# A fixed order on TensorE for attention: scores of two heads over all tokens in one run, transposes and value products in runs between projections

## The chip, the cores and the metric

The kernel runs on one core of a Trainium2 chip. The metric is the device time of one execution in microseconds (us). Engines are named TensorE (PE in the profile, its weight loads PEld), VectorE (DVE), ScalarE (ACT), GpSimd (POOL) and SyncE (SP). The change moves work on TensorE and, through a list scheduler, on the others.

## What is computed

A decoder trunk of two layers over 512 tokens of width 1024. The first layer is a gated short convolution with its feed-forward part, the second an attention layer with its own. The change lies in the attention layer alone. Cut to that:

```python
def dilated_attention_mixer(x, positions, k_sh, v_sh, w_q, w_o):
    q = rope((x @ w_q).reshape(B, S, N_BRANCHES * N_HEADS, HEAD_DIM), positions)
    for g, (window, dilation) in enumerate(((128, 1), (512, 4), (2048, 16))):
        o, lse = dilated_branch(q[:, :, g], k_sh[:, :, g], v_sh[:, :, g], window, dilation)
    wts = softmax(stack(lses), axis=0)
    return (sum over branches of wts * o) @ w_o
```

Each of the three branches has 16 heads of 64. `dilated_branch` takes the scores of a query with the keys of its own residue class and window, masks them, and returns the softmax-weighted values and the log of the sum of exponentials. k and v come from the same hidden state by another normalisation gain and another weight matrix, `w_kv`. All is float32.

## The kernel before, in words

**Products in three parts.** A float32 product is made of three TensorE products: activations and weights are split in a high and a low part (`split`, L88 to L91: a cast `wh` on ScalarE, a subtraction `wl` on VectorE), and high by high, high by low and low by high are added up in PSUM. `load` (L95) fetches 1 MB of weight into a tile `raw` of a pool with two buffers; `parts` (L101) multiplies it in place by the norm's gain (L110, VectorE, in two pieces per half, so four per `raw`), then splits it. `wh` and `wl` have six buffers each.

**The projections.** `feature_mm` (L119, matmul L137) runs 24 steps for a pair of outputs, 48 matmuls of 512 columns. `rope_mms` (L534) does this for q and for k of one branch, four heads at a time, and `rope` (L518) turns the result: eight narrow ScalarE copies `sw` (L527, L528), and three VectorE steps per output (L529 to L531). `sw` takes one of four buffers of tag "t".

**The heads.** There are four groups of four heads. A group's `Heads` object (L553) has these steps:
- `scores` (L568): fp32 matmuls q by k of 64 rows for two token blocks and both heads of a pair, into two PSUM banks of tag "at" (L580); a VectorE operation adds the mask, writes p and takes the maximum (L588); after the second two blocks `nm` (L595) and the exp on ScalarE (L598). `part` 1 holds branches 1 and 2, which share a token order, `part` 0 holds branch 0.
- `values` (L636): the projection v of one branch in two pieces of 48 matmuls of 256 columns each (L649), then copies to SBUF on ScalarE (L657, L662), 16 narrow ones for branch 0.
- `factors` (L601): the statistics of the two parts go through DRAM to the other part's token order and back (GpSimd DMAs, L612 to L616); VectorE makes the common maximum `mx` (L624) and from it the factor `f` (L625 to L633).
- `transposed` (L667): VectorE scales p by f (L676), TensorE transposes 128 x 128 tiles `tr` (L679), ScalarE copies them to `trs` (L681), again of tag "t".
- `times_v` (L684): fp32 value products into one bank `o` for both heads (L708), later copied out (L717).
- `units` (L721): per head pair, part and two token blocks a unit, that is a transposition of both heads; the products of a unit follow one unit later (`rest`).

**What sets the order.** The group loop (L749) does the six projection pairs of a group, builds the scores as a list `todo`, makes the six value pieces, then puts the units in `todo`. `fill` (L744) takes two items off the list: it is called after each value piece, so that scores stand between values, and after each projection pair, so that the units of a group stand between the projections of the next. The last group's units stand between steps of the output projection (`wo_step`, L505, `token_mm`, L175). PSUM has eight banks, four of tag "mm" for projections, values and output, four of tag "at". A scheduler then puts each engine's instructions in a row by a simulated time line, keeping data dependencies, buffers and the edges set with `tc.issue_after`; in this version it is free to cut a run of scores or transposes and put full-array matmuls between.

Of the kernel before, what the change touches and what calls it, by code (L numbers as in the profile page):

```python
# [38 lines left out]
def trunk(  # L39
# [78 lines left out]

    def feature_mm(jobs, t0, t1, attn):  # L119
# [12 lines left out]
        if t1 - t0 < NT:  # L132

            todo.sort(key=lambda kp: kp[1])
        for i, (k, p) in enumerate(todo):
            for ps, (_, (wh, wl)) in zip(outs, jobs):
                nc.tensor.matmul(ps, (wh, wl, wh)[p][:, k, :], x[p == 2][:, k],  # L137
                                 start=i == 0, stop=i == len(todo) - 1)

# [7 lines left out]

    def feature_mms(makers, between=None, attn=False, marks=((), ())):

# [3 lines left out]
        if between is None:  # L153
            pairs = [m() for m in makers]
            for i in range(0, len(pairs), 2):
                feature_mm(pairs[i:i + 2], 0, NT, attn)
            return [ps for ps, _ in pairs]
# [16 lines left out]

    def token_mm(outs, ah, al, wh, wl, first, last):  # L175
# [327 lines left out]

    def wo_step(k, tt, n):
        wh, wl = ws[4 * n + k // 2]  # L505
        return token_mm([ys[tt][n]], xh[:, tt, k, :], xl[:, tt, k, :],
                        [wh[:, k % 2, :]], [wl[:, k % 2, :]], k == 0, k == KT - 1)

    with ExitStack() as inner:
# [24 lines left out]
        def rope_mms(g, i, rest, fill):  # L534
# [4 lines left out]
            for src, gain in ((w_q[0], gq), (w_kv, gkv)):  # L539
                tag = "at" if ms and rest else "mm"  # L540
                ms += makers(tag, load_cols(src, c0), gain)
                if not rest:
                    d += [rope(ps, f"qk{g}", g) for ps in feature_mms(ms[-2:], None, True)]
                    fill()
# [8 lines left out]
        class Heads:  # L553
# [13 lines left out]

            def scores(self, part, pr, b2):  # L568

                st = self.st[part]  # L570
                ps = [bank("at", "s").rearrange("p (b k) -> p b k", b=2) for _ in range(2)]
                for b in (b2, b2 + 1):
                    for e in range(2):
# [4 lines left out]
                        for h2 in range(2):  # L578
                            rw = slice(64 * h2, 64 * h2 + 64)
                            nc.tensor.matmul(  # L580
                                ps[h2][:, b - b2, e * P:(e + 1) * P],
                                q[pr][rw, b * P:(b + 1) * P], k[pr][rw, kb * P:(kb + 1) * P],
                                start=True, stop=True)
                    lo = 128 if part == 0 and b == 0 else 0
                    mask = (maskA, maskB)[part]
                    for h2 in range(2):
                        hh = 2 * pr + h2
                        nc.vector.tensor_tensor_reduce(  # L588
                            self.p(part, hh, b), ps[h2][:, b - b2, lo:], mask[:, lo:],
                            1.0, -3.0e38, ALU.add, ALU.max, st[:, b, hh, 0:1])  # L590
                if b2 == 0:
                    return
                for hh in (2 * pr, 2 * pr + 1):
# [42 lines left out]
            def values(self, g):  # L636
# [7 lines left out]
                def piece(n):  # L644
                    for k in range(KT):
                        wh, wl = (x[:, k % 4, :] for x in w[k // 4])
                        for p in range(3):
                            for m in range(2):
                                nc.tensor.matmul(  # L649
                                    ps[m][:, n, :], (zh, zh, zl)[p][:, k, 2 * m + n],  # L650
                                    (wh, wl, wh)[p],
                                    start=k == 0 and p == 0, stop=k == KT - 1 and p == 2)
                    if n:
# [13 lines left out]
            def transposed(self, pr, part, hh, b2):  # L667
# [5 lines left out]
                for b in (b2, b2 + 1):  # L673
# [4 lines left out]
                    for e in range(lo, 256, P):  # L678
                        nc.tensor.transpose(  # L679
                            tr[:, b - b2, e:e + P], p[:, e - lo:e - lo + P], ident)  # L680
                nc.scalar.copy(trs.rearrange("p a b -> p (a b)")[:, lo0:], trf[:, lo0:])  # L681
                return trs

            def times_v(self, pr, part, b2, trs):  # L684
# [4 lines left out]
                o = self.o[pr]  # L689
                mark = None  # L690
                for b in (b2, b2 + 1):
                    for e in range(2):
                        if part == 0 and b + e == 0:
                            continue
                        for hh in range(2):
# [10 lines left out]
                            first = new and b == 0 and e == 0  # L706
                            with tc.issue_after(mark) if mark else nullcontext():
                                m = nc.tensor.matmul(  # L708
                                    out, v, rhs, start=first, stop=part == 0 and e == 1,
                                    skip_group_check=True).ins  # L710
                            if first:
                                mark = m
                if part == 1 or b2 == 0:
# [7 lines left out]
            def units(self):  # L721

                def unit(pr, part, b2):
# [5 lines left out]
                return [lambda a=(pr, part, b2): unit(*a)  # L729
                        for pr in range(2) for part in (1, 0) for b2 in (0, 2)] + [self.rest]  # L730

            def rest(self):
                what, trs = self.flight.pop(0)
                self.times_v(*what, trs)

# [8 lines left out]
        def fill():  # L744
            for f in todo[:2]:
                f()
            del todo[:2]

        for i in range(NG):  # L749
            qk = [rope_mms(g, i, pending.rest() if i == 0 and g == 0 else {}, fill)  # L750
                  for g in range(NB)]
            for f in todo:
                f()
# [4 lines left out]
            todo = [lambda a=(part, pr, b2): heads.scores(*a)  # L758
                    for part in range(2) for pr in range(2) for b2 in (0, 2)]
            for g in range(NB):  # L760
                for piece in heads.values(g):
                    piece()
                    fill()
            heads.factors()
            todo = heads.units()
        load_wo(0)
# [4 lines left out]
        steps = [(k, tt) for k in range(6) for tt in range(NT)]  # L771
        for n, f in enumerate(todo):
            for s in steps[3 * n:3 * n + 3]:
                wo_step(*s, 0)
            f()
# [79 lines left out]
```

## Time and profile before

| what | before |
|---|---|
| runs (three), median | 1523.56 us |
| lowest and highest run | 1521.35 and 1524.08 us |
| profiled execution: its time, its span | 1523.93 us, 1522.1 us |
| mean granted TensorE clock | 0.994 of full speed |
| TensorE busy | 1495.3 us (98%), 8158 matmul records |
| VectorE busy | 745.4 us (49%) |
| ScalarE busy | 616.4 us (40%) |
| GpSimd busy | 108.1 us (7%) |
| DMA | 137.43 MB, mean 90 GB/s |

The span is the part of the execution between the first and the last instruction that the profiler records. Matmuls overlap in the array, so a row's duration is longer than its distance to the next row, and times below are taken from start to start. An fp32 matmul (scores, value products) leaves two records, any other one. Lines named L... are those of the kernel before.

### The profile page before, as it was taken

What the parts mean: (1) busy time and instruction counts of PE and PEld (TensorE: products, weight loads), DVE (VectorE), ACT (ScalarE), POOL (GpSimd) and SP (SyncE); (2) the same over time, 40 slices, a digit from 0 to 9 for tenths busy, and PEclk for the clock granted to TensorE, in tenths of its full rate; (3) what the DMA queues carried; (4) which work ended last, traced back from release to release, by engine and by line L of the source; (5) the groups of instructions that cost most, each with busy time, mean ns of one, the idle gap of its engine ahead of it and who ended that gap; (6) DMA issues with size and microseconds to landing.
All of it is one profiled execution on the core that took longest, in us unless ns stands there. A gap on an engine that the chain in (4) does not pass through costs nothing.

```text
span 1522.1 us, 20115 instructions
## 1 busy us (share of the span) xinstructions
PE 1495.3 (98%) x8158; PEld 1262.2 (83%) x8158; DVE 745.4 (49%) x1328; ACT 616.4 (40%) x1137; POOL 108.1 (7%) x247
## 2 busy tenths in 40 slices
PE   8999999999999998999999999999998999999997
PEld 7888888888888887898788889889877888888886
DVE  5644453323234366776667566765554322223333
ACT  4323342212123244664666557557553221212321
POOL 2000320000000051000001001000023000000001
PEclk9999999999999999999999999999999999999999
DMA  6333123133323312322112222212040323332311
GB/s 210 111 112 110 56 94 127 62 106 111 124 87 107 111 38 74 111 85 80 61 58 85 84 73 69 84 56 84 30 138 24 124 76 111 111 109 99 111 56 56
DMA packets 109330, 137.43 MB, mean 90 GB/s; under 512 B 3469, under 2 KB 97973, under 8 KB 109238
## 3 DMA queue, kind: packets, MB, share of 16 engines
q1 hardware_dynamic: 107958, 135.89, 27.1%
q8 instruction: 64, 1.05, 0.3%
q0 software_dynamic: 1280, 0.26, 0.2%
q14 instruction: 28, 0.23, 0.0%
HBM read 133.92 MB, written 2.23 MB: 89 GB/s over the span
## 4 chain that ended last, share of the span: by engine, by line
PE 68%; issue 24%; POOL 5%; DVE 1%; ACT 1%; DMA 0%; SPq 0%; DVEq 0%; ACTq 0%; POOLq 0%
PE mmf L137 27%; PE atf L137 14%; PE vps L649 10%; PE s L580 3%; PE o L708 2%; PE tr L679 2%; POOL t L203 1%; POOL a L197 1%; POOL yi L205 1%; POOL q L204 1%; POOL t L206 1%; PE y L182 1%; PE y L180 1%; PE y L178 1%; DVE hn L228 0%
## 5 line engine op out<-in xcount | busy, mean ns | idle before, releaser
L91 DVE TENSOR_TENSOR wl<-raw,wh 128x1024 fp32r<-128x1024 f32 x244 | 292.7, 1222 | 70.7 <-ACT wh L90 70.4
L90 ACT CAST wh<-raw 128x1024 fp32r<-128x1024 f32 x244 | 246.7, 1047 | 100.7 <-PE atf L137 43.1
L137 PE MATMUL mmf<-xh,wh 128*128 128x512 f32 (+1 forms) x848 | 277.4, 380 | 0.2 <-ACT xh L90 0.2
L137 PE MATMUL mmf<-xl,wh 128*128 128x512 f32 (+1 forms) x848 | 271.2, 374 | 0.0
L137 PE MATMUL mmf<-xh,wl 128*128 128x512 f32 (+1 forms) x848 | 271.0, 374 | 0.0
L137 PE MATMUL atf<-xh,wh 128*128 128x512 f32 (+1 forms) x560 | 181.8, 368 | 0.0
L137 PE MATMUL atf<-xl,wh 128*128 128x512 f32 (+1 forms) x560 | 180.1, 365 | 0.0
L137 PEld LDWEIGHTS mmf<-xh,wh 128*128 128x128 f32 x848 | 154.7, 191 | 30.6 <-issue 2.1
L137 PE MATMUL atf<-xh,wl 128*128 128x512 f32 (+1 forms) x560 | 180.0, 365 | 0.0
L362 DVE TENSOR_TENSOR act<-atf,s 128x512 f32<-128x512 f32 x44 | 30.5, 692 | 304.1 <-ACT s L361 304.1
L137 PEld LDWEIGHTS mmf<-xl,wh 128*128 128x128 f32 x848 | 153.2, 188 | 28.8 <-issue 0.9
L137 PEld LDWEIGHTS mmf<-xh,wl 128*128 128x128 f32 x848 | 153.5, 189 | 27.7
L361 ACT ACTIVATE s<-mmf 128x512 f32<-128x512 f32 x44 | 26.3, 598 | 336.3 <-PE mmf L137 336.3
L110 DVE TENSOR_TENSOR raw<-raw,cols 128x512 f32<-128x512 f32 x144 | 90.2, 686 | 78.6 <-DMA raw<-in_w_kv 56.2
L137 PEld LDWEIGHTS atf<-xh,wh 128*128 128x128 f32 x560 | 100.6, 191 | 17.0
L137 PEld LDWEIGHTS atf<-xl,wh 128*128 128x128 f32 x560 | 99.6, 189 | 16.8
L137 PEld LDWEIGHTS atf<-xh,wl 128*128 128x128 f32 x560 | 99.5, 189 | 16.8
L527 ACT COPY sw<-mmf 32x512 f32<-32x512 f32 x92 | 53.3, 579 | 79.4 <-PE mmf L137 72.2
L649 PE MATMUL vps<-wh,xh 128*128 128x256 f32 x384 | 81.1, 289 | 0.0
L649 PE MATMUL vps<-wh,xl 128*128 128x256 f32 x384 | 79.3, 286 | 0.0
L649 PE MATMUL vps<-wl,xh 128*128 128x256 f32 x384 | 79.1, 285 | 0.0
L91 DVE TENSOR_TENSOR al<-act,ah 128x512 fp32r<-128x512 f32 x44 | 30.2, 691 | 93.9 <-ACT ah L90 93.9
(192 smaller groups left out, 2058.6 us busy)
## 6 DMA issues: line engine op xcount, KB each, us to landing
raw<-in_ffn_w_gate_up SPq DMA_DIRECT2D x44, 1024.0 KB, 7.5
raw<-in_w_kv SPq DMA_DIRECT2D x24, 1024.0 KB, 5.2
raw<-in_ffn_w_down SPq DMA_DIRECT2D x22, 1024.0 KB, 4.9
raw<-in_conv_w_in SPq DMA_DIRECT2D x12, 1024.0 KB, 5.2
raw<-in_w_q SPq DMA_DIRECT2D x12, 1024.0 KB, 5.2
raw<-in_conv_w_out SPq DMA_DIRECT2D x4, 1024.0 KB, 4.8
raw<-in_w_o SPq DMA_DIRECT2D x4, 1024.0 KB, 5.0
h<-in_x SPq DMA_DIRECT2D x4, 512.0 KB, 8.9
```

The lines of the kernel that those rows point to most:

```text
L90: return [nc.scalar.copy(hi, src).ins, nc.vector.tensor_tensor(lo, src, hi.bitcast(F32), ALU.subtract).ins]
L91: nc.vector.tensor_tensor(lo, src, hi.bitcast(F32), ALU.subtract).ins]
L110: nc.vector.tensor_tensor(src[:, ks], src[:, ks], g.broadcast_to([P, a // 2, b]), ALU.mult)
L137: nc.tensor.matmul(ps, (wh, wl, wh)[p][:, k, :], x[p == 2][:, k], start=i == 0, stop=i == len(todo) - 1)
L178: nc.tensor.matmul(o, ah, wh[i], start=first, stop=False)
L361: nc.scalar.activation(s, ps[2 * j], AF.Silu)
L362: nc.vector.tensor_tensor(act[2 * c + j], ps[2 * j + 1], s, ALU.mult)
L527: nc.scalar.copy(w[s:s + 32], y[s + 32:s + 64])
L580: nc.tensor.matmul(ps[h2][:, b - b2, e * P:(e + 1) * P], q[pr][rw, b * P:(b + 1) * P], k[pr][rw, kb * P:(kb + 1) * P], start=True, stop=True)
L649: nc.tensor.matmul(ps[m][:, n, :], (zh, zh, zl)[p][:, k, 2 * m + n], (wh, wl, wh)[p], start=k == 0 and p == 0, stop=k == KT - 1 and p == 2)
L679: nc.tensor.transpose(tr[:, b - b2, e:e + P], p[:, e - lo:e - lo + P], ident)
L708: m = nc.tensor.matmul(out, v, rhs, start=first, stop=part == 0 and e == 1, skip_group_check=True).ins
```

## The change

1. `strict` issues a TensorE instruction and adds an edge from the strict one issued before it. All of the projections with `fill`, the scores, value pieces, transposes, value products and the output steps between the last units go through it, so that TensorE keeps the order in which the program is written. (All those instructions then bear line L124.)
2. `scores` does all four token blocks of a head pair in one go, 14 matmuls for part 0 and 16 for part 1, and takes all four banks of tag "at" for it.
3. `fill` takes one item instead of two. It is called ahead of each value piece instead of behind it, and also in the middle of each projection pair, ahead of its 25th matmul.
4. A unit's transposes are made one unit at a time, and value products in pairs of units: before an even unit's transposes come the products of the two units before.
5. `token_mm`, where it is strict, does the three products of an output in a row.

Cut to its core:

```diff
+    traced = []
+    def strict(op, *args, **kwargs):
+        with tc.issue_after(traced[0]) if traced else nullcontext():
+            traced[:] = [op(*args, **kwargs).ins]
...
+    def feature_mm(jobs, t0, t1, attn, fill=None):
...
         for i, (k, p) in enumerate(todo):
+            if fill and i == len(todo) // 2:
+                fill()
             for ps, (_, (wh, wl)) in zip(outs, jobs):
...
+                if fill:
+                    strict(nc.tensor.matmul, *args, **kwargs)
...
-            def scores(self, part, pr, b2):
+            def scores(self, part, pr):
...
-                ps = [bank("at", "s").rearrange("p (b k) -> p b k", b=2) for _ in range(2)]
-                for b in (b2, b2 + 1):
+                banks = [[bank("at", "s").rearrange("p (b k) -> p b k", b=2) for _ in range(2)]
+                         for _ in range(2)]
+                for b in range(NT):
...
-                    self.flight.append(((pr, part, b2), [
-                        self.transposed(pr, part, hh, b2) for hh in (2 * pr, 2 * pr + 1)]))
-                    if len(self.flight) > 1:
+                def unit(n, what):
+                    if n % 2 == 0:
                         self.rest()
+                    if what:
+                        pr, part, b2 = what
+                        self.flight.append((what, [
+                            self.transposed(pr, part, hh, b2) for hh in (2 * pr, 2 * pr + 1)]))
...
             def rest(self):
-                what, trs = self.flight.pop(0)
-                self.times_v(*what, trs)
+                for what, trs in self.flight:
+                    self.times_v(*what, trs)
+                self.flight.clear()
...
         def fill():
-            for f in todo[:2]:
-                f()
-            del todo[:2]
+            if todo:
+                todo.pop(0)()
...
             for g in range(NB):
                 for piece in heads.values(g):
+                    fill()
                     piece()
-                    fill()
```

How the order of instructions changes is shown at three places. In these rows `s<-qk` is a score, `vps` a value matmul, `mmf` a projection matmul, `tr` a transpose of p, `o<-trs` a value product; "x6" is six alike in a row, and numbers behind a name tell tiles apart.

TensorE, the score phase of the third group, before (the first rows lie in the second value piece):

```order
L649 MATMUL vps<-wh,xl 128x256 x2
L649 MATMUL vps<-wh,xh 128x256
L580 MATMUL s<-qk_6750,qk_6623 128x128 x6
L649 MATMUL vps<-wh,xh 128x256
L649 MATMUL vps<-wl,xh 128x256 x2
L649 MATMUL vps<-wh,xl 128x256 x2
L580 MATMUL s<-qk_6759,qk_6632 128x128
L649 MATMUL vps<-wh,xh 128x256 x2
```

After, from the last projection matmul to the value piece behind the second run:

```order
L124 MATMUL mmf<-xl,wh 128x512 x2
L124 MATMUL s<-qk_6774,qk_6641 128x128 x14
L124 MATMUL vps<-wh,xh 128x256 x2
...
L124 MATMUL vps<-wh,xl 128x256 x2
L124 MATMUL s<-qk_6783,qk_6650 128x128 x14
L124 MATMUL vps<-wh,xh 128x256 x2
```

The scores of a head pair were cut into several runs with value matmuls between them; now the 14 stand together, with a whole value piece behind them. Over the four groups, 51 score runs have become 16.

TensorE, the first units of the third group, before:

```order
L137 MATMUL mmf<-xh,wh 128x512 x2
L679 MATMUL tr<-ident,p_7256 128x128 x16
L137 MATMUL mmf<-xh,wl 128x512 x2
...
L137 MATMUL mmf<-xh,wl 128x512 x2
L708 MATMUL o<-trs,v_7478 64x128 x2
L708 MATMUL o<-trs,v_7673 64x128 x2
L708 MATMUL o<-trs,v_7478 64x128 x2
L708 MATMUL o<-trs,v_7673 64x128 x2
L137 MATMUL mmf<-xl,wh 128x512 x2
...
L137 MATMUL mmf<-xl,wh 128x512 x2
L679 MATMUL tr<-ident,p_7255 128x128 x3
L137 MATMUL mmf<-xh,wh 128x512 x2
```

After:

```order
L124 MATMUL mmf<-xl,wh 128x512 x2
L124 MATMUL tr<-ident,p_7256 128x128 x8
L124 MATMUL mmf<-xh,wh 128x512 x2
...
L124 MATMUL mmf<-xl,wh 128x512 x2
L124 MATMUL tr<-ident,p_7256 128x128 x8
L124 MATMUL mmf<-xh,wh 128x512 x2
...
L124 MATMUL mmf<-xl,wh 128x512 x2
L124 MATMUL o<-trs,v_7478 64x128 x2
L124 MATMUL o<-trs,v_7673 64x128 x2
...
L124 MATMUL o<-trs,v_7673 64x128 x2
L124 MATMUL tr<-ident,p_7255 128x128 x6
```

Each unit's eight transposes now stand by themselves, half a projection pair apart, and the products of two units stand together (two times 16 records), directly followed by the next transposes. The first transposes come 24 projection matmuls after the last value matmul.

VectorE, behind the last `nm` of the second group, before:

```order
L110 TENSOR_TENSOR raw_6952<-raw_6952,cols_73 128x4x128 [waits DMAHW4_49]
L110 TENSOR_TENSOR raw_6952<-raw_6952,cols_73 128x4x128 x3
L91 TENSOR_TENSOR wl_6820<-raw_6816,wh_6819 128x1024 [waits Activation_49]
L91 TENSOR_TENSOR wl_6827<-raw_6816,wh_6826 128x1024 [waits PE_49,Activation_49]
L624 TENSOR_TENSOR mx_6531<-st0_6000,ot0_6517 128x16 [waits DMASW2_49,DMASW3_49,DMASW1_49,DMASW0_49]
L624 TENSOR_TENSOR mx_6545<-st1_6001,ot1_6518 128x16 [waits DMASW6_49]
L625 TENSOR_TENSOR ea_6532<-st0_6000,mx_6531 128x16 [waits DVE_49]
...
L629 TENSOR_TENSOR f0_6534<-ea_6532,st0_6000 128x16 [waits Activation_49]
```

After:

```order
L91 TENSOR_TENSOR wl_6681<-raw_6677,wh_6680 128x1024 [waits Activation_49]
L91 TENSOR_TENSOR wl_6688<-raw_6677,wh_6687 128x1024 [waits PE_49,Activation_49]
L110 TENSOR_TENSOR raw_6943<-raw_6943,cols_73 128x4x128 [waits DMAHW4_49,DVE_49]
L110 TENSOR_TENSOR raw_6943<-raw_6943,cols_73 128x4x128 x2
L644 TENSOR_TENSOR mx_6531<-st0_6000,ot0_6517 128x16 [waits DMASW2_49,DMASW3_49,DMASW1_49,DMASW0_49]
L644 TENSOR_TENSOR mx_6545<-st1_6001,ot1_6518 128x16 [waits DMASW6_49]
L110 TENSOR_TENSOR raw_6943<-raw_6943,cols_73 128x4x128
L91 TENSOR_TENSOR wl_6814<-raw_6810,wh_6813 128x1024 [waits Activation_49]
...
L646 TENSOR_TENSOR eb_6547<-ot1_6518,mx_6545 128x16
```

Here `raw_6943` is the weight loaded into the buffer of `raw_6677`, after `wl_6688` has read that. Three of its four gain pieces now stand between `wl_6688` and `mx`, and the fourth with a `wl` between `mx` and `ea`; before, `mx` came right behind the two `wl`.

## Rows read from the trace of the kernel before

**Rows 1.** Windows view: stretch, length, busy by engine (records), clock, DMA.

```profile
639.88:770.61 130.73, 130.73 (x877) 111.18 (x876) 89.42 (x213) 80.20 (x173) 6.08 (x10) 1.00 0.25 78
900.04:947.52 47.48, 47.48 (x409) 44.37 (x408) 33.26 (x101) 34.44 (x97) 3.77 (x7) 1.00 0.23 73
947.52:1029.54 82.02, 82.02 (x471) 66.64 (x469) 53.92 (x110) 45.15 (x75) 2.13 (x4) 1.00 0.23 75
1029.54:1077.02 47.48, 47.48 (x410) 44.18 (x408) 25.72 (x87) 36.80 (x100) 4.59 (x8) 1.00 0.23 74
```

**Rows 2.** Timeline of TensorE, scores among value matmuls: start, busy us, instruction, count.

```profile
917.54 0.72 PE L580 MATMUL s<-qk,qk 64*128 64x128 f32 x8
918.19 0.38 PE L649 MATMUL vps<-wh,xh 128*128 128x256 f32 x1
...
920.57 0.40 PE L649 MATMUL vps<-wl,xh 128*128 128x256 f32 x2
920.89 1.16 PE L580 MATMUL s<-qk,qk 64*128 64x128 f32 x16
921.99 0.50 PE L649 MATMUL vps<-wh,xl 128*128 128x256 f32 x2
922.33 0.40 PE L649 MATMUL vps<-wh,xh 128*128 128x256 f32 x2
```

**Rows 3.** Timeline of TensorE, transposes and value products among projection matmuls.

```profile
958.89 1.91 PE L679 MATMUL tr<-ident,p 128*128 128x128 f32 x16
960.56 0.71 PE L137 MATMUL mmf<-xh,wl 128*128 128x512 f32 x2
...
968.81 0.61 PE L137 MATMUL mmf<-xh,wl 128*128 128x512 f32 x2
969.36 1.09 PE L708 MATMUL o<-trs,v 128*64 128x128 f32 x16
970.38 0.73 PE L137 MATMUL mmf<-xl,wh 128*128 128x512 f32 x2
970.95 0.62 PE L137 MATMUL mmf<-xh,wh 128*128 128x512 f32 x2
...
987.05 1.04 PE L679 MATMUL tr<-ident,p 128*128 128x128 f32 x8
```

**Rows 4.** Timeline of VectorE; in brackets the idle time before, and its releaser.

```profile
910.46 0.42 DVE L588 CUSTOM_DVE_ANT_0 p<-s,cst 128x256 f32<-128x256 f32 x1
...
951.19 0.26 DVE L624 TENSOR_TENSOR mx<-st,ot 128x16 f32<-128x16 f32 x2 [0.30 <-DMA ot<-d]
...
952.97 3.37 DVE L676 TENSOR_SCALAR p<-p,f 128x128 f32<-128x128 f32 x13
...
991.83 0.69 DVE L529 TENSOR_TENSOR qk<-mmf,cos 128x512 f32<-128x512 f32 x1 [0.35 <-ACT sw L528]
...
994.77 1.22 DVE L91 TENSOR_TENSOR wl<-raw,wh 128x1024 fp32r<-128x1024 f32 x1
...
1001.24 2.50 DVE L110 TENSOR_TENSOR raw<-raw,cols 128x512 f32<-128x512 f32 x4 [5.25 <-DMA raw<-in_w_kv]
```

**Rows 5.** Timeline of ScalarE: V copies, exp, casts of weights, trs copies.

```profile
918.64 3.75 ACT L662 COPY v<-vps 32x256 f32<-32x256 f32 x10
...
943.72 0.49 ACT L598 ACTIVATE p<-p,nm 128x256 f32<-128x256 f32 x1
...
963.15 2.00 ACT L90 CAST wh<-raw 128x1024 fp32r<-128x1024 f32 x2
965.17 1.08 ACT L681 COPY trs<-tr 128x512 f32<-128x512 f32 x2
```

**Rows 6.** TensorE after an idle time, and two stretches of the windows view.

```profile
1146.69 0.90 PE L236 MATMUL tr<-ident,hn 128*128 128x128 f32 x3 [3.91 <-DVE hn L228]
```

```profile
1146.50:1149.90 3.40, 3.21 (x14) 2.99 (x15) 3.40 (x7) 1.79 (x4) 1.19 (x3) 0.50 0.02 5
1098.00:1113.20 15.20, 14.66 (x141) 11.68 (x139) 0.69 (x1) 6.54 (x13) 0.00 (x0) 1.00 0.07 27
```

More of the change, by code (lines that the diff above doesn't have):

```diff
@@ L135, in feature_mm @@
         for i, (k, p) in enumerate(todo):
+            if fill and i == len(todo) // 2:
+                fill()
             for ps, (_, (wh, wl)) in zip(outs, jobs):
-                nc.tensor.matmul(ps, (wh, wl, wh)[p][:, k, :], x[p == 2][:, k],
-                                 start=i == 0, stop=i == len(todo) - 1)
+                args = ps, (wh, wl, wh)[p][:, k, :], x[p == 2][:, k]
+                kwargs = {"start": i == 0, "stop": i == len(todo) - 1}
+                if fill:
+                    strict(nc.tensor.matmul, *args, **kwargs)
+                else:
+                    nc.tensor.matmul(*args, **kwargs)
     @contextmanager
@@ L146, in behind, with feature_mms @@
             yield
-    def feature_mms(makers, between=None, attn=False, marks=((), ())):
+    def feature_mms(makers, between=None, attn=False, marks=((), ()), fill=None):
         half = NT // 2
@@ L173, in makers, with token_mm @@
                 for j in range(2)]
-    def token_mm(outs, ah, al, wh, wl, first, last):
+    def token_mm(outs, ah, al, wh, wl, first, last, strictly=False):
+        if strictly:
+            for i, o in enumerate(outs):
+                strict(nc.tensor.matmul, o, ah, wh[i], start=first, stop=False)
+                strict(nc.tensor.matmul, o, ah, wl[i], start=False, stop=False)
+                strict(nc.tensor.matmul, o, al, wh[i], start=False, stop=last)
+            return
         for i, o in enumerate(outs):
@@ L542, in rope_mms @@
                 if not rest:
-                    d += [rope(ps, f"qk{g}", g) for ps in feature_mms(ms[-2:], None, True)]
+                    d += [rope(ps, f"qk{g}", g) for ps in feature_mms(
+                        ms[-2:], None, True, fill=fill)]
                     fill()
@@ L579, in scores @@
                             rw = slice(64 * h2, 64 * h2 + 64)
[L580 to L583, printed above, removed]
+                            strict(nc.tensor.matmul,
+                                   banks[b // 2][h2][:, b % 2, e * P:(e + 1) * P],
+                                   q[pr][rw, b * P:(b + 1) * P], k[pr][rw, kb * P:(kb + 1) * P],
+                                   start=True, stop=True)
+                for b in range(NT):
                     lo = 128 if part == 0 and b == 0 else 0
@@ L588, in scores @@
                         nc.vector.tensor_tensor_reduce(
-                            self.p(part, hh, b), ps[h2][:, b - b2, lo:], mask[:, lo:],
+                            self.p(part, hh, b), banks[b // 2][h2][:, b % 2, lo:], mask[:, lo:],
                             1.0, -3.0e38, ALU.add, ALU.max, st[:, b, hh, 0:1])
-                if b2 == 0:
-                    return
                 for hh in (2 * pr, 2 * pr + 1):
@@ L648, in piece @@
                             for m in range(2):
[L649 to L652, printed above, removed]
+                                strict(nc.tensor.matmul,
+                                       ps[m][:, n, :], (zh, zh, zl)[p][:, k, 2 * m + n],
+                                       (wh, wl, wh)[p],
+                                       start=k == 0 and p == 0, stop=k == KT - 1 and p == 2)
                     if n:
@@ L706, in times_v @@
                             first = new and b == 0 and e == 0
[L707 to L712, printed above, removed]
+                            strict(nc.tensor.matmul, out, v, rhs, start=first,
+                                   stop=part == 0 and e == 1, skip_group_check=True)
                 if part == 1 or b2 == 0:
@@ L751, in trunk @@
                   for g in range(NB)]
-            for f in todo:
-                f()
+            while todo:
+                fill()
             if pp is None:
@@ L757, in trunk @@
             heads = Heads(i, qk)
-            todo = [lambda a=(part, pr, b2): heads.scores(*a)
-                    for part in range(2) for pr in range(2) for b2 in (0, 2)]
+            todo += [lambda a=(part, pr): heads.scores(*a)
+                     for part in range(2) for pr in range(2)]
             for g in range(NB):
                 for piece in heads.values(g):
+                    fill()
                     piece()
-                    fill()
             heads.factors()
-            todo = heads.units()
+            todo += heads.units()
         load_wo(0)
```

23 lines of the change are left out of this document (10 added, 13 removed).

## The prediction

> **What bounds the kernel now.** I read the page's busy table first: TensorE is busy nearly throughout, so the time is TensorE's row of instructions laid end to end. Then I cut the attention into stretches [rows 1]. From 900.04 to 947.52 and from 947.52 to 1029.54, the two parts of the third head group, TensorE's busy time equals the stretch: nothing is waited for, at full clock. VectorE and ScalarE are busy for 33.3 and 34.4 us of the first 47.5, and for 53.9 and 45.2 of the next 82.0; they have slack on the average, which says nothing about one moment. What a changed order can save is the price of switching on TensorE; what it can lose is a wait where there is none now.
>
> I call a run of small instructions between two full-array matmuls a detour. Its price is the time between the full matmuls beyond their own pace (0.120 us each with 256 columns, 0.227 with 512, from the steps between rows that hold nothing else [rows 2, 3]).
>
> **Scores.** From 920.57 to the row at 922.33 lie four value matmuls (0.48) and 16 score records, eight fp32 matmuls [rows 2]: the detour costs 1.76 - 0.48 = 1.28. Eight records last 917.54 to 918.19 = 0.65 and 16 last 920.89 to 921.99 = 1.10, so a record costs 0.45/8 = 0.056, and the switch there and back 1.28 - 16 x 0.056 = about 0.39. The first stretch of the third group holds 288 value matmuls (34.56) in 47.48, which leaves 12.9 for its scores; the last group's stretch is as long [rows 1]. The changed order has four runs per group with 120 records: 4 x 0.39 + 120 x 0.056 = 8.3. Saved: 4.6.
>
> **Transposes and value products.** Sixteen transposes last 958.89 to 960.56 [rows 3], with the way back 0.11 each, with hardly a price for switching. Sixteen product records cost 970.95 - 968.81 - 4 x 0.227 = 1.23; at a score record's price 0.35 of it is the switch. The second stretch holds 288 projection matmuls (65.4) in 82.02, so its detours cost 16.6 [rows 1]. In the new order stand 60 transposes (6.6), 120 records (6.6) and four switches (1.4): 14.6. Saved: 2.0.
>
> That is 6.6 per group, 26.4 for four. The first group is 130.73 long against 129.50 for the third [rows 1], which I put down to more splintered scores, so 1.2 more: **27.6 saved**. For the last group, whose transposes lie between output-projection steps, I take the same 2.0; from nothing to twice that moves the sum by 2 either way. No instruction is added or removed on any engine, and no DMA.
>
> **The wait before the first transposes.** Call the end of a group's last projection 0. TensorE then does four score runs (8.3), six value pieces of 48 matmuls (34.6) and, now ahead of any transpose, half a projection pair (24 x 0.227 = 5.4): it reaches the first transposes at 48.3. They want scaled p, p wants the factor f, and f wants mx. The chain on the other engines:
> - The projection before the last ended at -10.9 (48 x 0.227), and its second wl ends 8.9 after it, as 987.05 (a projection's end) to 994.77 + 1.22 = 995.99 shows [rows 3, 4]: -2.0. The next weight lands 5.25 later [rows 4]: 3.3.
> - VectorE then does a gain in four pieces (2.5), four rope steps at 0.7, two wl at 1.2 and four reductions at 0.35 [rows 4], which brings the first nm to about 12.5.
> - ScalarE's queue behind that nm holds 32 exps, four casts wh, 16 narrow V copies and two wide ones up to the cast that lets the raw buffer go. At 0.49 an exp, 1.0 a cast, 0.375 a narrow and 0.54 a wide copy (priced as a trs copy) [rows 5] that is 15.7 + 4.0 + 6.0 + 1.1 = 26.8. It runs without a gap, since TensorE delivers scores and values sooner: 39.3. The wl behind it ends at 40.5, and the next weight lands 5.25 later, at 45.8.
> - In VectorE's new order three gain pieces of that weight stand ahead of mx; before, mx came right behind wl. So mx starts at 45.8 + 1.9 = 47.7 at the earliest. mx to the end of f takes 1.8 (951.19 to 952.97), and between them now stand the fourth gain piece (0.6) and two wl (2.4); then come three scalings of part 0 and the first of part 1, 4 x 0.26 [rows 4]. The first transpose can go at 53.5.
>
> The wait is 53.5 - 48.3 = **5.2** in each of the first three groups. Bounds: nothing, if the chain is 5 us shorter (an in-order queue of 40 us summed by hand can be off by that), and 10, if as much longer. Without the gain pieces mx would be in time: it comes 7.0 after the last exp's end, 944.21 to 951.19 [rows 4, 5], at about 43. In the last group no projection follows; its transposes stand behind casts of the output weights, for between 0 and 5.2, and I take 2.6. Sum: 3 x 5.2 + 2.6 = **18.2**.
>
> **The wait inside the value products.** The rope's sw and the copied transposes trs share four buffers. The order is now transposes of an even unit, half a projection, transposes of the odd unit, half a projection, products of both. The odd unit's second trs copy takes the buffer that the even unit's products free, and these now come immediately ahead of the odd unit's products. So TensorE stops inside each pair of products for the copy (1.08/2 = 0.54 [rows 5]) and two hand-overs, about 0.3. In one place of four the buffer comes from a rope add, and I take a little more there: 0.9 on the mean, between 0.54 and 1.2. Four in each of three groups: **10.8**. Before, projections lay between and hid the copy.
>
> In the score phase the four banks of a run are released by reductions during the 5.8 us of the value piece that follows. With VectorE 70% busy there [rows 1] I price this at nothing; where that cover fails it costs up to 1 us at 12 places.
>
> [...]
>
> **Sum**, against the profiled execution's 1523.93, which is 0.4 above the median of the runs: 1523.93 - 27.6 + 18.2 + 10.8 + 5.1 = **1530.4**. A measurement of this kernel can tell about 0.2%, 3.0 us, from no change, so this is slower by twice that.
>
> **Rivals.**
> 1. *The waits are there, but smaller by a third, or the clock does not fall*: 1530.4 - 6.1 = 1524.3 or 1530.4 - 5.1 = 1525.3, no change. For it: there is one such stop in the trace to take the clock's fall from. Chance 0.22.
> 2. *No wait at the first transposes* (the other side). It decides at 48.3 of a group: if the weight lands by about 40, so that mx and f are done in time, TensorE goes on. For it: VectorE and ScalarE have 30% slack [rows 1]; against it: mx is queued behind a load that needs ScalarE's whole queue drained. Then 1530.4 - 18.2 - 5.1 = 1507.1, faster. Half the wait, with no fall of the clock, gives 1530.4 - 9.1 - 5.1 = 1516.2, faster too. Chance of either 0.32.
> 3. *The clock falls at the value products as well*, twelve times 1.7: 1530.4 + 20.4 = 1550.8. Against it stands that in 1098 to 1113.2, a mix of transposes, products and output steps, the clock stayed at 1.00 [rows 6]. [...] Chance 0.08.
> 4. *The change does not do what it says*, the order staying splintered: the instruction order shows 16 score runs of 14 or 16 matmuls, so no chance is left for this.
>
> **How the numbers follow.** The forecast, waits of about 5 us with the clock falling, has 0.38, rival 1 0.22, rival 2 0.32, rival 3 0.08. Slower by over 0.2% is the forecast without a lower edge of 0.03, and rival 3: 0.43. Same: 0.22 + 0.03 = 0.25. Faster: 0.32. The range goes down to rival 2's far end, 1507, and up to 1540, the forecast with first waits of 8.4 (3 x 3.2 = 9.6 more); it leaves out rival 3 and some of the ends, about 0.2. The likeliest case's own range is 1525 to 1540.
>
> **What would show it.** In the changed profile each group should have 8.3 us of score detours, and one idle stretch of about 5 us before its first tr, ended by VectorE's p, with VectorE's gain waiting for its load ahead of mx. Inside each pair of value products an idle piece of 0.5 to 1.2 us should end on ScalarE's trs. A granted clock of 0.50 should follow each long wait, and nothing else that is new. I am wrong if the first transposes start without a wait (the chain is shorter than summed), if score runs wait for their banks, or if the detours cost as much as before, because a switch from head to head inside a run costs what one between runs did.

## The result, and the profile after

The changed kernel takes 1535.19 us (median of four runs, 1534.69 to 1536.28) against 1522.64 for the kernel before in the same comparison: a ratio of 1.0083, 95% interval 1.0066 to 1.0101. It is slower, as forecast, and inside the range; the forecast itself was 1530.4. The profiled execution of the changed kernel took 1536.28 us with a span of 1534.5, 12.4 more than before in either.

Did the runs come together, and at what price? Windows view of the changed kernel (stretch, length, busy by engine with counts, granted clock, DMA share, GB/s). The first three rows are the first three head groups, from the first score run to the next group's first; then four stretches behind a wait; then the units of the third group.

```profile
638.83:775.05 136.22, 127.14 (x877) 110.36 (x876) 89.85 (x213) 80.48 (x174) 6.06 (x10) 0.97 0.23 72
775.05:909.24 134.19, 126.58 (x877) 109.82 (x877) 86.84 (x210) 79.43 (x173) 5.88 (x10) 0.99 0.23 72
909.24:1043.85 134.61, 127.66 (x877) 110.62 (x876) 87.01 (x210) 79.39 (x173) 5.88 (x10) 0.97 0.22 71
...
694.90:699.00 4.10, 4.06 (x15) 3.61 (x16) 4.10 (x17) 1.17 (x2) 0.00 (x0) 0.56 0.51 178
828.87:832.40 3.53, 3.53 (x14) 3.21 (x15) 3.53 (x14) 1.17 (x2) 0.00 (x0) 0.62 0.73 254
962.94:968.12 5.18, 5.18 (x17) 4.41 (x17) 5.18 (x21) 1.17 (x2) 0.00 (x0) 0.50 0.49 170
1089.90:1094.90 5.00, 4.74 (x17) 3.89 (x18) 5.00 (x18) 1.66 (x3) 0.00 (x0) 0.66 0.00 0
970.00:1043.00 73.00, 71.42 (x418) 58.07 (x417) 43.14 (x61) 41.66 (x66) 0.00 (x0) 1.00 0.18 59
```

Before, TensorE filled its stretches [rows 1]. Now each group lasts 4.8 to 5.5 us longer, although TensorE is busy for less: 127.7 us in the third against 129.5. It lacks 7 to 9 us of work per group. The saving is there, and more than that is spent on waiting. What it waited for stands in the waits view (engine, tile and line, releaser: us in all, times, longest; "issue" says that the view shows no releaser):

```profile
PE tr L124 <- DVE p L696: 11.1, 3, 5.5
...
PE tr L124 <- issue: 7.5, 1, 7.5
...
PE o L124 <- ACT trs L701: 3.9, 6, 1.2
PE y L124 <- ACT v L677: 1.8, 1, 1.8
```

The wait of 7.5 is that of the first group. Its VectorE rows show the same order as in the others: mx behind the gain pieces of a late load, and the first scaling of p at 693.84, 1.1 before the first transpose at 694.94.

Here are the places on TensorE, in the third group; the first transposes, a unit without a wait, and two rows of a product pair in the second group:

```profile
909.24 1.83 PE L124 MATMUL s<-qk,qk 64*128 64x128 f32 x28
911.00 0.50 PE L124 MATMUL vps<-wh,xh 128*128 128x256 f32 x2
...
956.96 0.61 PE L124 MATMUL mmf<-xl,wh 128*128 128x512 f32 x2
962.94 1.97 PE L124 MATMUL tr<-ident,p 128*128 128x128 f32 x8 [5.37 <-DVE p L696]
964.56 1.20 PE L124 MATMUL mmf<-xh,wh 128*128 128x512 f32 x2
965.56 1.05 PE L124 MATMUL mmf<-xh,wl 128*128 128x512 f32 x2
...
987.16 1.04 PE L124 MATMUL tr<-ident,p 128*128 128x128 f32 x8
987.96 0.71 PE L124 MATMUL mmf<-xh,wh 128*128 128x512 f32 x2
...
858.39 2.63 PE L124 MATMUL o<-trs,v 128*64 128x128 f32 x28
860.95 1.09 PE L124 MATMUL tr<-ident,p 128*128 128x128 f32 x8
```

In the last group the wait stands at an output step y. TensorE's row, and under it the casts and the copies of ScalarE that it waited for:

```profile
1089.95 0.50 PE L124 MATMUL y<-wh,xh 128*128 128x512 f32 x1 [1.85 <-ACT v L677]
...
1086.31 3.10 ACT L90 CAST xh<-O 128x512 fp32r<-128x512 f32 x3
1089.31 1.07 ACT L677 COPY v<-vps 128x512 f32<-128x512 f32 x2
```

The 28 score records (14 matmuls) last 1.76, in place of several detours [rows 2]. The first transposes start 5.37 after TensorE was ready, and run at half the clock: 1.62 for eight, where a later unit needs 0.80. The 28 product records and the way on take 2.56, which by record and switch should be 1.9.

In ScalarE's and VectorE's rows of the third group one reads why p was late. Timeline of VectorE:

```profile
948.43 1.23 DVE L91 TENSOR_TENSOR wl<-raw,wh 128x1024 fp32r<-128x1024 f32 x1 [0.82 <-ACT wh L90]
955.64 1.90 DVE L110 TENSOR_TENSOR raw<-raw,cols 128x512 f32<-128x512 f32 x3 [5.98 <-DMA raw<-in_w_kv]
957.45 0.25 DVE L644 TENSOR_TENSOR mx<-st,ot 128x16 f32<-128x16 f32 x2
957.62 0.68 DVE L110 TENSOR_TENSOR raw<-raw,cols 128x512 f32<-128x512 f32 x1
...
961.88 4.42 DVE L696 TENSOR_SCALAR p<-p,f 128x128 f32<-128x128 f32 x17
```

Three gain pieces wait 5.98 us for the weight that the wl at 948.43 made room for, and mx comes behind them; before, mx came at 951.19 without a gain piece ahead of it, 0.30 after VectorE was free [rows 4]. TensorE is ready at 957.5, 48.3 after the group's first score at 909.24, as forecast, and goes on at 962.9, 53.7 after it, against 53.5.

Summed, against the forecast:

| term | forecast | measured, and where |
|---|---|---|
| score runs | -19.6 | -19.4: all score detours 52.7 before, 33.3 after |
| transposes and products, without waits | -8.0 | -7.7: 66.6 before, 58.9 by record and switch after |
| wait at the first transposes, groups 1 to 3 | +15.6 | +18.4: 7.5, 5.5, 5.4 |
| last group | +2.6 | +2.0: 1.85 at an output step, 0.2 at the transposes |
| stops inside product pairs | +10.8 | +11.9: 3.8, 4.3, 3.8 |
| low clock | +5.1 | +7.4: the four stretches above, length by missing share |
| sum | +6.5 | +12.6, against 12.4 measured |

Detour prices are the time between full matmuls beyond their own pace, as in the prediction, and without the wait of 0.9 that both kernels have behind the last product.

### The profile page after: what moved, and what is told of

It reads as the page before. It is cut to its first block, busy times and chain, and to the rows that moved or that the text cites. A ratio compares the mean times of both kernels' runs of the same rounds, so it can differ in the third digit from the quotient of the medians.

```text
span 1534.5 us, 20143 instructions
## 1 busy us (share of the span) xinstructions
PE 1482.0 (97%) x8158; PEld 1257.9 (82%) x8158; DVE 743.7 (48%) x1328; ACT 616.0 (40%) x1137; POOL 107.0 (7%) x247
## 5 line engine op out<-in xcount | busy, mean ns | idle before, releaser
L151 PE MATMUL mmf<-xh,wh 128*128 128x512 f32 (+1 forms) x496 | 163.7, 369 | 0.1
L151 PE MATMUL mmf<-xl,wh 128*128 128x512 f32 (+1 forms) x496 | 160.5, 362 | 0.0
L151 PE MATMUL mmf<-xh,wl 128*128 128x512 f32 (+1 forms) x496 | 160.5, 362 | 0.0
L124 PE MATMUL mmf<-xh,wh 128*128 128x512 f32 x352 | 113.3, 403 | 0.0
L124 PE MATMUL mmf<-xh,wl 128*128 128x512 f32 x352 | 109.6, 393 | 0.0
L124 PE MATMUL mmf<-xl,wh 128*128 128x512 f32 x352 | 109.0, 391 | 0.0
L151 PEld LDWEIGHTS mmf<-xh,wh 128*128 128x128 f32 x496 | 89.8, 194 | 16.3 <-ACT xh L90 1.7
L151 PEld LDWEIGHTS mmf<-xh,wl 128*128 128x128 f32 x496 | 87.7, 189 | 14.5
L151 PEld LDWEIGHTS mmf<-xl,wh 128*128 128x128 f32 x496 | 87.5, 189 | 14.2
L546 ACT COPY sw<-mmf 32x512 f32<-32x512 f32 x92 | 53.2, 578 | 109.9 <-PE mmf L124 98.8
L124 PE MATMUL vps<-wh,xh 128*128 128x256 f32 x384 | 79.0, 287 | 0.0
```

The source lines that it names most:

```text
L124: traced[:] = [op(*args, **kwargs).ins]
L151: nc.tensor.matmul(*args, **kwargs)
L546: nc.scalar.copy(w[s:s + 32], y[s + 32:s + 64])
```

## The experiments

In each comparison the kernel before was run anew, with medians of 1522.4 to 1523.3 us. Behind each ratio stands its 95% interval.

**1. The gain behind the scalings.** The forecast's own claim: mx is late because of what stands ahead of it.

```diff
-                    nc.vector.tensor_scalar(
-                        p, p, self.fs[part][:, b, hh:hh + 1], None, ALU.mult)
+                    fmark[:] = [nc.vector.tensor_scalar(
+                        p, p, self.fs[part][:, b, hh:hh + 1], None, ALU.mult).ins]
...
+                    with behind(fmark if g == 1 and n == 1 else []):
                         d += [rope(ps, f"qk{g}", g) for ps in feature_mms(
```

> Edit: on VectorE the four gain pieces of the weight for k of the second branch are queued behind the scalings of p, so that mx no longer stands behind that weight's load. Theory A (the first transposes wait because mx is queued behind the gain, and the gain behind a load): the three waits of 7.5, 5.5 and 5.4 us and the low clock after each go, 8.7 + 6.7 + 6.6 us of detour price in the changed kernel; 1535.2 - 22 = about 1513, with the first transposes of a group starting within 0.5 us of the matmul ahead of them. Rival B (f is late for another reason, the DMA trip of the statistics or the load itself): the wait stays at 3 us or more per group and the time at 1525 or above.

Measured: 1526.09, ratio 1.0027 [1.0017, 1.0038]. Theory A and rival B were both partly right: the price of the first transposes beyond their own fell from 8.7, 6.7 and 6.6 to 6.5, 1.9 and 2.8, and did not go. The timeline shows what is late next: the last exp on ScalarE, mx on VectorE, SyncE's load of the weight, and the two halves of the statistics' trip through DRAM on GpSimd:

```profile
938.64 0.49 ACT L620 ACTIVATE p<-p,nm 128x256 f32<-128x256 f32 x1
...
950.09 0.26 DVE L646 TENSOR_TENSOR mx<-st,ot 128x16 f32<-128x16 f32 x2 [6.62 <-DMA ot<-d]
...
943.50 0.37 SPq L98 DMA_DIRECT2D raw<-in_w_kv  x1
...
939.52 0.76 POOL L635 DMA_DIRECT2D d<-st  x1 [10.64 <-ACT p L620]
943.23 2.19 POOL L637 DMA_DIRECT2D ot<-d  x4 [2.95 <-DMA d<-st]
```

mx now waits for the statistics, which set out at 939.5 and are back at 950.1, 11.0 after the last exp's end at 939.1. In the third group of the kernel before it was 7.0 [rows 4, 5].

**2. The units later.** The same wait, without touching VectorE's order.

```diff
-            todo += heads.units()
+            todo += [lambda: None] * (1 if i < NG - 1 else 0) + heads.units()
```

> Edit: the order on VectorE is left alone, but the first fill behind a group's value pieces is empty, so that TensorE reaches the first transposes half a projection pair (5.4 us) later. Theory A: waits of 7.5, 5.5 and 5.4 become 2, 0 and 0, the clock falls at most once, and the time is 1535.2 - 20 = about 1515. Rival B (the pause belongs to the switch to transposes and moves with it): nothing gained, 1533 or more.

Measured: 1511.19, ratio 0.9932 [0.9916, 0.9949]; better than the 1515 that theory A gave. The first transposes' waits are 1.9 us in the first group and at most 0.6 in the others; that of the third group:

```profile
947.46 1.23 PE L124 MATMUL tr<-ident,p 128*128 128x128 f32 x8 [0.64 <-DVE p L696]
```

But the stops inside the product pairs shrank as well, from four in each group to one, of 0.8, 2.3 and 2.3. The unit that had its transposes at a projection's end is now the even one, whose copies have half a projection more time. That was the first sign that more than the buffer was at work in these stops.

**3. Products one unit at a time.**

```diff
-                    if n % 2 == 0:
-                        self.rest()
+                    self.rest()
```

> Edit: the products of a unit come ahead of the next unit's transposes, one unit at a time, as before the change, instead of in pairs; all else as changed. Theory A (the odd unit's second trs copy waits for the buffer that the even unit's products free, and the products wait for the copy): the stops of 0.84 to 1.75 inside the pairs, 11.8 us in all, go, and 12 more switches at 0.35 cost 4.2: 1535.2 - 7.6 = about 1527.5. Rival C (what is lost inside a pair is the switch from one unit's products to the next on the same bank, not a wait): it stays, and the time is 1535 to 1540.

Measured: 1532.49, ratio 1.0074 [1.0059, 1.0089]; a gain of 2.7, not 7.6. The switches cost 4.5, near the 4.2 priced, and smaller stops remained at four of a group's eight products: about 0.2, 0.46, 0.24 and 0.53. ScalarE shows why, at the one that was due at 888.21:

```profile
884.94 0.58 ACT L547 COPY sw<-mmf 32x512 f32<-32x512 f32 x1
885.54 2.00 ACT L90 CAST wh<-raw 128x1024 fp32r<-128x1024 f32 x2
887.57 1.07 ACT L701 COPY trs<-tr 128x512 f32<-128x512 f32 x2
```

The trs copies stand behind the rope's copies and two casts.

**4. The first and the third together.**

> Edits of the first and the third run together. Theory A: the savings add up, 1535.2 - 22 - 7.6 = about 1505.5, faster than the kernel before by about 1.1%. Rival D (without its waits TensorE runs into the next limit, a late load or a late rope): a new wait of some us per group appears, and the time is 1512 to 1520.

Measured: 1521.71, ratio 0.9995 [0.9986, 1.0004]. The gain of 13.5 is a little more than the two edits gave alone (9.1 and 2.7), and far from the 29.6 that theory A promised. The waits at the first transposes are still 5.1, 1.8 and 2.0.

**5. The load after mx.** Why did the statistics take 11 us in the first run?

```diff
+                    mxmark[:] = [nc.vector.tensor_tensor(mx, ma, mb, ALU.max).ins]
...
-        split(wh, wl, src)
+        with behind(late):
+            split(wh, wl, src)
```

(`late` is `mxmark` for the second half of the weight for k of the first branch, and empty otherwise.)

> Edit, on top of the first run (gain behind the scalings): the second wl of the weight for k of the first branch is queued behind mx, so that the next 1 MB weight load, which waits for that wl, starts only when the statistics are back. Theory E (in the first run mx came 11.0 us after the last exp, against 7.0 in the kernel before, because the 4 KB transfers of the statistics went beside the 1 MB load): mx comes about 7 us after the last exp; the waits that the first run still had, 6.5, 1.9 and 2.8 us of detour price, become 3.5, 0 and 0: 1526.1 - 7.7 = about 1518.4. Rival F (the trip takes 11 us whatever goes beside it): mx stays 11 us behind the last exp, and the time at 1526 or above.

Measured: 1521.18, ratio 0.9987 [0.9978, 0.9997], 2.8 above what theory E gave. The weight's load now starts behind mx. Last exp, mx and load:

```profile
936.19 0.49 ACT L621 ACTIVATE p<-p,nm 128x256 f32<-128x256 f32 x1
...
944.63 0.27 DVE L647 TENSOR_TENSOR mx<-st,ot 128x16 f32<-128x16 f32 x2 [5.66 <-DMA ot<-d]
...
946.06 0.37 SPq L98 DMA_DIRECT2D raw<-in_w_kv  x1
```

mx comes 7.95 after the last exp's end instead of 11, and the price of the first transposes falls to 5.7, less than 0.1, and 0.9. Theory E holds for the trip: from the last exp's end to mx it is 9.2, 10.0 and 11.0 us in the three groups of the first run, where the 1 MB load starts in between, and 6.3, 6.7 and 8.0 here, where it starts behind mx. That is 3 us in each group. In the third group the way out takes 3.7 and 3.9 in the two runs; the way back, which the load goes beside in the first run alone, takes 6.9 against 3.6. What makes the trip longer beside a load, the two runs do not show. In the first group 4.4 us of wait remain. There the last exps begin late (in the first run at 674.74, with ScalarE idle for 3.9 us before, for an nm that stands behind two gain pieces on VectorE), which looks like the same pattern once more; no run moved that nm alone.

**6. The score part alone.** The transposes and products left to the scheduler, as before; scores, values and projections as changed.

> One part of the change alone: merged and fixed score runs, value pieces and projections in fixed order; the transposes and value products are left to the scheduler, two units per fill and none in the middle of a projection pair, as before. If the parts are independent: scores cost 33.3 instead of 52.7 us, transposes and products 67 as before, and the time is 1522.4 - 19.4 = about 1503. If the end of the chain over mx sets the first transposes here too (theory A), waits of 1 to 5 us at the first transposes remain, and the time is 1505 to 1518.

Measured: 1512.71, ratio 0.993 [0.9913, 0.9946]. The score detours cost 33.6, as in the whole change, so that saving stands by itself; transposes and products rose from 67.5 to 75.0 (with the 0.9 behind the last product), 3.4 of it at the first transposes of the three groups (1.0, 1.2, 1.3), whose chain ends late here too. In the second and third group transposes also wait 0.8 for a trs copy; the rest is not traced. So this half of the change is worth 10 us, and the other half, the fixed place of the units, costs 22 on top of it.

**7. Four buffers for trs.** The buffer theory by itself: sw goes into O, the tile that gathers the attention's output, where that isn't in use yet.

```diff
-            sw = tp.tile([P, T], F32, tag="t", name="sw")
+            swn.append(g)
+            sw = (O[:, 4 + len(swn) % 2, :] if i in (1, 2)
+                  else tp.tile([P, T], F32, tag="t", name="sw"))
```

> Edit on the changed kernel: in the second and third group's projections the rope's sw lies in two tiles of O that are not yet in use, so that the trs copies of the first and second group's units have all four buffers; the third group's units share them with sw as in the change. Theory A (buffer): the stops inside the product pairs go in the first two groups, 3.8 + 4.3 us, and the third keeps its 3.8: 1535.2 - 8.1 = about 1527. Rival C (switch or bank): all three groups keep theirs, 1535.

Measured: 1532.27, ratio 1.0061 [1.0046, 1.0076], a gain of 2.9 of the 8.1. In the first two groups the stops go from 0.84, 0.84, 1.2 (or 1.75), 0.89 to 0.58, 0.85, 0.64, 0.87; the third keeps its own. So the buffer made four of the eight stops longer, by 0.3 to 1.1; the rest is something else (run 9).

**8. Four edits together.** Later units, the gain behind the scalings, the load after mx, sw in O.

> Edits together: units half a projection pair later (second run), gain behind the scalings (first run), load after mx (fifth), sw in O (seventh). From the second run's 1511.2: its first waits of 3.0, 0.6 and 1.0 go to about 1 in all, and of its stops in product pairs (0.8, 2.3, 2.3) the first two go: 1511.2 - 3.5 - 3.1 = about 1504.5. If the units' new place has already taken what these edits give, 1509 to 1512.

Measured: 1508.81, ratio 0.9902 [0.9887, 0.9917]. That is in the rival's range of 1509 to 1512, not the 1504.5 hoped for. The first transposes hardly wait any more (0.4 at most). New waits of 0.5 and 1.0 for a trs copy stand at the fourth unit's transposes of the first two groups, and the third group got a new stop, of 3.9, in its first product pair:

```profile
958.91 1.19 ACT L708 COPY trs<-tr 128x512 f32<-128x512 f32 x2 [2.45 <-DVE qk L556]
...
959.55 2.57 PE L125 MATMUL o<-trs,v 128*64 128x128 f32 x16 [3.91 <-ACT trs L708]
```

Its sw tiles still share the four buffers, and the rope add that frees them (qk, L556) came late on VectorE, behind eight gain pieces, scalings of p and two wl.

**9. The casts behind the trs copies**, on top of the seventh run.

```diff
+                    with behind(hist.get(c - 3, ())):
+                        ready = [m() for m in ms[-2:]]
```

(`hist` holds the last trs copy of each projection's odd unit; the casts that came ahead of it are those of the third projection on.)

> Edit, on top of the seventh run (sw out of the trs buffers in the first two groups' units): on ScalarE the two casts of a weight are queued behind the trs copies of an odd unit, not ahead of them. Theory G (the odd unit's transposes come at a projection's end, where eight sw copies, 4.7 us, and two casts, 2.0, stand ahead of its trs copies, together more than the 5.4 us until the products): the stops of 0.58, 0.85 and 0.64 in each of the first two groups fall to 0.2 or less, the fourth (0.86), where the casts are those of a value weight and stay ahead, remains; 1532.3 - 4 = about 1528. Theory A alone (buffers): nothing is left to gain, 1532.

Measured: 1529.92, ratio 1.0041 [1.0025, 1.0057]. In the first two groups the first three stops are gone (below 0.1 each) and the fourth stayed (0.87 and 0.88), both as theory G had it; the time is 1.9 above its 1528. No run moves the casts with the buffers left as they were, so what the casts alone are worth stays open. ScalarE's and TensorE's rows, and under them those of the changed kernel at a pair:

```profile
838.49 1.07 ACT L711 COPY trs<-tr 128x512 f32<-128x512 f32 x2
839.45 2.01 ACT L90 CAST wh<-raw 128x1024 fp32r<-128x1024 f32 x2
...
840.15 1.09 PE L124 MATMUL o<-trs,v 128*64 128x128 f32 x16
```

```profile
851.97 1.04 PE L124 MATMUL tr<-ident,p 128*128 128x128 f32 x8
851.98 0.58 ACT L546 COPY sw<-mmf 32x512 f32<-32x512 f32 x1 [4.75 <-PE mmf L124]
...
856.72 2.00 ACT L90 CAST wh<-raw 128x1024 fp32r<-128x1024 f32 x2
858.74 1.13 ACT L701 COPY trs<-tr 128x512 f32<-128x512 f32 x2
```

In the change the odd unit's transposes are done by 853, and its trs copies start at 858.74, after the products were due at 858.39 (TensorE's row above): eight sw copies and two casts, 6.7 us, stand between.

**10 and 11. Two sums of edits.** Run 10: later units, sw in O also in the last group's first branch, and in the last group the later casts of O behind the value copies. Run 11: in addition the gain behind the scalings and the load after mx.

```diff
+            with behind(vmark if k > 2 else ()):
+                heads_x(k, O[:, k, :])
```

> Edits together: units half a projection pair later (second run); sw in two tiles of O wherever these are free, also in the first branch of the last group; in the last group the casts of the last three tiles of O queued behind the last value copies, for which the output projection waited 1.85 us. From the second run's 1511.2: stops in product pairs of 0.8, 2.3 and 2.3 go, and the output step's wait with its low clock, about 2.3: about 1503.5. If the freed work only moves the wait to the next late copy, 1508 or more.

> The run before, and in addition the gain behind the scalings and the load after mx (first and fifth run). The first waits that the second run still had, 3.0, 0.6 and 1.0, go to 2.3 in all: about 1501.5. If the load that now starts later is missed further on, a new wait in the second half of the projections and 1504 or more.

Measured: run 10 takes 1509.35, ratio 0.9906 [0.989, 0.9923], run 11 1502.08, ratio 0.9861 [0.9846, 0.9875]. In both the stops inside the pairs and the output step's wait are gone. In run 10 the waits at the first transposes came back, 3.1 and 3.4 us in the second and third group. TensorE is there no sooner than in run 2 (53.8 after the third group's first score in both); the chain is later. The last nm starts 37.3 after the first score, behind gain pieces of a late load, against 34.6 in run 2, and mx, still behind the next gain, 53.2 against 50.5. Why that load is later stays open. Rows of run 10:

```profile
928.58 1.29 DVE L110 TENSOR_TENSOR raw<-raw,cols 128x512 f32<-128x512 f32 x2 [3.38 <-DMA raw<-in_w_q]
...
931.68 0.23 DVE L620 TENSOR_SCALAR nm<-st 128x4 f32<-128x4 f32 x2
...
945.18 2.50 DVE L110 TENSOR_TENSOR raw<-raw,cols 128x512 f32<-128x512 f32 x4 [4.81 <-DMA raw<-in_w_kv]
947.60 0.25 DVE L649 TENSOR_TENSOR mx<-st,ot 128x16 f32<-128x16 f32 x2
...
951.52 0.69 PE L124 MATMUL tr<-ident,p 128*128 128x128 f32 x2 [3.35 <-DVE p L701]
```

That is why run 10 ended where its expectation had the wait only move (1508 or more). Run 11 has these waits out of the way and came within 0.6 of the 1501.5 expected. From 700 to 1090 TensorE is busy for 386.8 of 390.0 us at full clock, and of the waits on attention tiles this is left:

```profile
PE tr L125 <- ACT trs L709: 2.6, 3, 1.0
...
PE tr L125 <- DVE p L704: 0.6, 1, 0.6
```

It is 1.4% faster than the kernel before and 2.2% faster than the change.

## Why the prediction was right, and where it was not

- **What a run saves.** Right: four runs at 0.39 and 120 records at 0.056 were to cost 8.3 per group, and cost 8.3; transposes and products 14.6, and 14.5 without their stops (the 120 product records at 0.056 are 6.7, not the 6.6 summed there). Bundling pays what the switches cost, and the sixth run shows it alone.
- **The first transposes.** Right in place, about in size, and in the chain: in the third group wl ended 40.4 after the first score (40.5 summed), the gain started at 46.4 (45.8), mx at 48.2 (47.7) and the first transpose at 53.7 (53.5). A wait of 5.2 was forecast, 5.5 and 5.4 came in two groups, and 7.5 in the first, where I had taken the other groups' sum. The cause named was half of it: without the gain ahead of mx (run 1) waits of 5.3, 1.5 and 2.5 remain, half of the 18.4, and with the load behind mx too (run 5) 4.4, 0 and 0.6. Wrong was the sentence that without the gain pieces mx would be in time, 7.0 after the last exp: run 1 waited 11 for it, and run 5, at 8, shows most of the difference to be the weight's own load beside it. So theory A's 22 us were not to be had with one edit.
- **The stops inside products.** The size was right (10.8 against 11.9) and the reason only in part, so the size was partly luck. I put them down to the buffer; runs 3, 7 and 9 show that ScalarE's queue held most of them up by nearly as much with the buffers out of the way. Two causes lay over each other, the second just shorter than the first, and I stopped at the one I had found.
- **The clock.** No run shows the sum's 5.1, three times 1.7 for waits of 5.2 us: it was my estimate from a single idle time of 3.91 us, with 3.4 us at a clock of 0.50 behind it [rows 6]. In its place, the lower clock behind the waits of 7.5, 5.5 and 5.4 us (0.56, 0.62 and 0.50 on the mean of the stretches above) cost 1.8, 1.3 and 2.6 us. The term was too small mostly because of the last group: there a wait of 1.85 us was followed by a mean clock of 0.66 for 5 us, which I had not counted. That does not come each time: the same output step waited 1.84 us in run 1, with the same instructions behind it, and the clock stayed at 1.00. Rival 3 did not come: in 970 to 1043, with seven units' transposes, all of the group's products and their four stops, the clock stayed at 1.00.
- **The last group.** Taken as half a wait at the transposes; it was an output step waiting for a value copy that stood behind three casts of O on ScalarE, 1.85 us. Run 10 moves those casts behind and it is gone. That 2.0 is near the 2.6 forecast is luck.
- **The total.** The profiled execution came out 5.9 above the forecast's 1530.4: 2.8 in the first three groups' waits (2.3 of it in the first), 2.3 in the clock, 1.1 in the stops and 0.5 in the savings, less 0.6 in the last group; these terms overshoot by 0.2.

## What to carry to other kernels

A fixed order on one engine makes its own work cheaper and takes away its freedom to do something else while another engine is late; before fixing it, sum the chain of every other engine up to each point where the fixed order needs something, and leave that point later than the longest. A short operation on the way to such a point (here mx, behind gain pieces that waited 5.98 us, or nm, or a copy) must not stand in an in-order queue behind one that waits for a transfer. Take away one wait and look again: two causes can lie over each other, as the buffer and the copies' queue did here, and the second is worth an experiment of its own.

## What the runs showed of the hardware that was not expected

- The statistics' trip through DRAM (16 KB out, four transfers of 4 KB back) took 9.2 to 11.0 us from the last exp to mx when a 1 MB load started during it (run 1), and 6.3 to 8.0 when the load started behind it (run 5).
- Eight transposes behind a 5.4 us wait took 1.62 us instead of 0.80, and the granted clock was 0.50 for 5.2 us after TensorE went on (962.94 to 968.12).
- Stops of 0.8 to 1.75 us inside the products left the clock at 1.00 (in 836 to 908 and 970 to 1043). Behind a single wait of about 2 us the clock fell in one run and not in another: the last group's output step waited 1.85 us in the change, with a mean clock of 0.66 over the 5 us behind it, and 1.84 in run 1, with 1.00. Nor did it fall behind the 2.45 us ahead of the third group's first transposes in run 1 (1.00 as well). What decides it stays open. Windows view of run 1 behind its two waits:

```profile
1079.20:1084.20 5.00, 4.79 (x27) 3.66 (x27) 5.00 (x18) 1.56 (x3) 0.00 (x0) 1.00 0.00 0
953.80:958.80 5.00, 4.91 (x25) 4.07 (x26) 5.00 (x17) 1.11 (x2) 0.00 (x0) 1.00 0.00 0
```
